# Where the low parts of the FFN operands are made, and in which order its weights are loaded

## The chip, the cores and the metric

One core of a Trainium2 chip runs the whole program. The metric is device time in microseconds (us) of one execution. The engines are named as in the profile: PE (TensorE) multiplies, DVE (VectorE), ACT (ScalarE) and POOL (GpSimd) work element by element, and SP (SyncE) only issues DMAs; POOL issues some too, through a queue of its own.

## What is computed

A trunk of two layers on x (1024 tokens by 1024 features), float32. Layer 0 mixes tokens with a gated DeltaNet, layer 1 with dilated-window attention; behind each mixer stands a SwiGLU block. Scale, shift and gate of each half layer come from a conditioning vector c.

```python
mod = (cond @ w_ada[layer] + b_ada[layer])
sh1, sc1, g1, sh2, sc2, g2 = jnp.split(mod[:, None, :], 6, axis=-1)
h = rms_norm(x, norm_mix[layer]) * (1.0 + sc1) + sh1
y = gated_deltanet_mixer(h, ...) if layer % 2 == 0 else dilated_attention_mixer(h, ...)
x = x + g1 * y
h = rms_norm(x, norm_ffn[layer]) * (1.0 + sc2) + sh2
gate, up = jnp.split(h @ w_ffn_in[layer], 2, axis=-1)     # 1024 x 2816 each
x = x + g2 * ((jax.nn.silu(gate) * up) @ w_ffn_out[layer])
```

## The kernel before

**Split numbers.** A float32 operand is held as a high part, rounded to the PE's 32-bit format by a copy on ACT, and a low part, the difference. One product of such operands is three matmuls (`split3`, `PE.then`, line L82 in the profile). `lo_of` (L164) makes the low parts. It counts its calls, and while `lo_pool` is 2 every second one goes to POOL, the others to DVE. `lo_pool` is 0 during the gated DeltaNet and 2 from the late part of layer 0's output projection (L1389) to the end.

**FFN-in.** The hidden size 2816 is 22 tiles of 128 columns, each with a gate part and an up part; the tokens are two halves of 512. A tile's four products (gate and up, by two halves) are made by a scheme of the Strassen kind with seven products, x = 1 to 7 (class `FfnIn`). Each of the seven is twelve matmuls of 128x128 by 128x512: four blocks of the feature sum by three. Its two operands are sums and differences: on the token side B[1] to B[7], made once per layer in `half0` (B[1], B[2]: the first 512 tokens) and `half1` (B[3] to B[7], which need the second 512 tokens); on the weight side made per tile in `weights`. Each of the operands has a high and a low part. A product is made in one of the PSUM banks "u", "y" and "v" (FFN-out's in "pd"). `taken` copies a finished product out of PSUM and adds it up; `column` makes silu(gate) times up of the second half; results go to the DRAM array `a_d`.

**The order of the products.** `begin` runs x=1 and x=2 of tiles 0, 1 and 2, which need the first tokens only. Inside it, behind the last product of tile 1, the norm's sums of the second tokens are reduced (`factors`: a product with ones into "pt", DVE at L347, and a short Newton step); behind the first product of tile 2 the factors are spread over the partitions by another small product and a copy (`row_bcast`, "rb", ACT at L306). Then `half1` multiplies the eight blocks of the second half by the row (L1157), scales and shifts them (ACT L1158), and forms B[3] to B[7]: the differences at L1174 and L1181 on DVE, two groups of four differences in place at L1177 and L1183 on POOL, and twenty operands with a high part (ACT L1151) and a low part (L164). `rest` runs the other products: for x in 3, 7, 6, 5, 4 tile 0 and tile 1 in turn (ten products), then tile by tile 7, 6, 2, 5, x=1 of the next tile, 3, 4. Meanwhile, in layer 0, every second product is followed by a piece of layer 1's conditioning (`mods1`): a DMA of 128x512 of `w_ada` ("araw"), and a multiply-add on DVE at L228 or L230.

**Weights.** A tile's two weight blocks of 128x1024 come by SP's queue into four buffers "wraw" (L1193), first used at the tile's first product in the text. Tile 2's first block, needed early, is loaded into a buffer of its own, "wr" (L1209). Its high part is made at L1215. Differences of blocks are at L1225 (POOL), L1226 and L1229 (DVE), the high parts of weight operands at L1198. `begin` makes the operands of (0,3), (1,3), (0,7) and (1,7) ahead of their products.

**FFN-out** (`ffn_out`) reads `a_d` back (L1343), in groups of 2, 4, 4, 4, 4 and 4 tiles, splits it (ACT L1345, L164), loads w_ffn_out (L1321), and adds each product times the gate to x (L1358), which in the first group is loaded from `xs_d` (L1354).

**What sets the order.** A scheduler puts each engine's instructions in an order from dependences and an estimate of their times; PE's in `begin` and `rest` are pinned to the order of the text. Each engine, and each DMA queue, then works in that order and waits where an input or a buffer is missing. So an instruction that waits holds all behind it on its engine.

Of the kernel before, what the change touches and what calls it, by code (L numbers as in the profile page):

```python
# [71 lines left out]
def trunk(tc, A, out, stop=None):  # L72
# [85 lines left out]
    cnt = [0]  # L158
    lo_pool = 2

    def lo_of(o, x, hi):
        cnt[0] += 1
        e = G if lo_pool and cnt[0] % lo_pool == 0 else V
        e.tensor_tensor(o, x, hi.bitcast(F32), ALU.subtract)  # L164
# [371 lines left out]
    with ExitStack() as ga:  # L536
# [4 lines left out]
        w_in = A["gdn_w_in"][0]  # L541
        lo_pool = 0
        wpools()
# [589 lines left out]
    class FfnIn:  # L1133
# [32 lines left out]
        def half1(self, xs, rb):  # L1166
            x0, x1, ft, sums = self.x0, xs, self.ft, self.sums
            for k in range(4, KT):
                self.h(k, x1[k], rb)
                self.B[3].append(self.pair(x1[k], False))  # L1170
            for k in range(4):
                self.h(k, x1[k], rb)
                t = sums.take()
                V.tensor_tensor(t, x1[k + 4], x1[k], ALU.subtract)  # L1174
                self.B[7].append(self.pair(t, True))
                sums.give(t)
                G.tensor_tensor(x0[k], x1[k], x0[k], ALU.subtract)  # L1177
                ft.give(x1[k])
            for k in range(4):
                t = sums.take()  # L1180
                V.tensor_tensor(t, x1[k + 4], x0[k], ALU.subtract)  # L1181
                self.B[6].append(self.pair(t, True))
                G.tensor_tensor(x0[k + 4], x0[k + 4], t, ALU.subtract)  # L1183
                sums.give(t)
                ft.give(x1[k + 4])
            for x, far, ts in ((5, True, x0[:4]), (4, False, x0[4:])):
                for t in ts:
                    self.B[x].append(self.pair(t, far))
                    ft.give(t)

        def raw(self, c0):
            r = self.raws()
            SP.dma_start(r.rearrange("p (k n) -> p k n", k=KT), rows_cols(A["w_ffn_in"][self.l], c0, P))  # L1193
            return r

        def op(self, x):
# [5 lines left out]
        def weights(self, i, x):  # L1202
            s, ft = self.st[i], self.sums
            if x in (1, 2):
                if x == 1:
                    if i == 2:

                        r = self.fw.tile([P, 1024], F32, name="wr", tag="wo")
                        SP.dma_start(r.rearrange("p (k n) -> p k n", k=KT),  # L1209
                                     rows_cols(A["w_ffn_in"][self.l], i * P, P))  # L1210
                    else:
                        r = s["rg"] = self.raw(i * P)
                        s["ru"] = self.raw(HID + i * P)
                    w = s["w"] = wps.tile([P, 2, 1024], F32R, name="w", tag="w")
                    ACT.activation(w[:, 0], r, AF.Copy)  # L1215
                    lo_of(w[:, 1], r, w[:, 0])
                c = slice((x - 1) * HALF, x * HALF)
                return s["w"][:, 0, c], s["w"][:, 1, c]
            if "rg" not in s:
                s["rg"], s["ru"] = self.raw(i * P), self.raw(HID + i * P)  # L1220
            a11, a12, a21, a22 = (t[:, j * HALF:(j + 1) * HALF] for t in (s["rg"], s["ru"]) for j in range(2))
            if x in (6, 5, 3) and "s1" not in s:
                t = self.fw.tile([P, 2, HALF], F32, name="ss", tag="wo")
                s["s1"], s["s2"] = t[:, 0], t[:, 1]
                G.tensor_tensor(s["s1"], a21, a22, ALU.add)  # L1225
                V.tensor_tensor(s["s2"], s["s1"], a11, ALU.subtract)  # L1226
# [47 lines left out]
        def column(self, i, g, where, x):  # L1274
# [3 lines left out]
            G.tensor_tensor(t, t, g, ALU.mult)  # L1278
            SP.dma_start(a_d[i, 1], t)
            where.give(g)  # L1280
            self.ft.give(t)

        def begin(self, factors, bcast):

            for i in range(3):
                self.product(i, 1)
# [3 lines left out]
                if i == 1:  # L1290
                    r = factors()
                    for j in ((0, 3), (1, 3), (0, 7), (1, 7)):
                        self.ops[j] = self.weights(*j)
# [39 lines left out]
    def ffn_out(l, ft, fw, raws, tail, between=None):  # L1333
# [4 lines left out]
        for gi, gn in enumerate(FG):  # L1338
            wo, acts = [], [[], []]
            for t in range(t0, t0 + gn):  # L1340
                for hf in range(2):
                    r = ft.take()
                    SP.dma_start(r, a_d[t, hf])  # L1343
                    hi, lo = hl_tile()
# [5 lines left out]
            for hf in range(2):  # L1350
                for n in range(KT):
                    if gi == 0:
                        xT[hf].append(ft.take())
                        SP.dma_start(xT[hf][n], xs_d[hf, n])  # L1354
                    o = pd()
# [32 lines left out]

    lo_pool, accs, araw = 2, None, 2  # L1389
    with ExitStack() as fa:  # L1390
# [48 lines left out]
        for kind in (1, 2):  # L1439
            pre.update(attn_products(0, 0, kind, range(2), hT, bank["p%d" % kind],  # L1440
                                     attn_weights(0, 0, kind, lambda ap, a: wtwo(fw, raws(), ap, a))))
        wcyc[0] = cycle([(wps, 1, (fw, "wraw", 4))])
        pre["w"] = attn_weights(0, 0, 0)
# [22 lines left out]
    with ExitStack() as da:  # L1466
# [200 lines left out]
        def half_done(hf):  # L1667
# [17 lines left out]
            stat = [Stat(None, *tmp[0:2]), Stat(None, *tmp[2:4])]  # L1685
            wpools(dw, 2, 2, 4)
            for h2, ns in ((0, range(KT)), (1, range(3)), (1, range(3, KT))):
                for n in ns:
# [93 lines left out]
```

## Time and profile before

| | us |
|---|---|
| median of 3 runs (lowest, highest) | 3025.17 (3014.49, 3026.26) |
| the profiled execution | 3023.1 |
| its span | 3021.3 |
| PE busy | 2799.0 |
| DVE busy | 1607.3 |
| ACT busy | 1067.9 |
| POOL busy | 998.1 |

In rows of windows each busy time is followed by the number of instructions; PEclk is the TensorE clock that was granted, as a share of full speed. The span is the time from the first to the last instruction of the profiled execution. An engine's busy time adds up its instructions. Stretches of the span by the profile: layer 0's late output projection and `begin` to the end of the ten products 820 to 935, its `rest` to 1330, its FFN-out 1330 to 1572; the same stages of layer 1 at 2280 to 2394, to 2750 and to the end, where the output phase overlaps the last products.

### The profile page before, as it was taken

Reading aid. Unit: us, or ns where it says so; the run is one execution under the profiler, and the core shown is the slowest. Engines: PE = TensorE matmul, PEld = TensorE weight load, DVE = VectorE, ACT = ScalarE, POOL = GpSimd, SP = SyncE. Lnnn points to the kernel's source line nnn. Section 1 sums busy time; section 2 is a strip of 40 time slices with the busy share of each in tenths; the row PEclk is TensorE's granted clock in tenths of the full one; section 3 lists DMA queues with packets and bytes.
Section 4 is the critical chain, followed back from the end, with each engine's and each line's share of the span. In section 5 each row is a group of like instructions: output and inputs, shape, how many; then the busy total and the mean of one; then the engine's idle time right before and its main releaser. Section 6 shows DMA issues by size and latency. Waiting matters only on the chain.

```text
span 3021.3 us, 40540 instructions
## 1 busy us (share of the span) xinstructions
PE 2799.0 (93%) x15303; PEld 2373.6 (79%) x15303; DVE 1607.3 (53%) x3055; ACT 1067.9 (35%) x2139; POOL 998.1 (33%) x866
## 2 busy tenths in 40 slices
PE   6889888898969999999999899999977899999999
PEld 5767777777757787877889799999966688887887
DVE  7875676656565555567455342333277633336443
ACT  5432333333443333332224453443335333334110
POOL 2141324332254343433224122322224633336220
PEclk8989999999989999999999999999968899999999
DMA  7333422236714433466212311111232222237211
GB/s 255 98 93 113 109 84 69 54 98 187 234 43 123 132 119 119 133 235 195 86 63 68 101 39 36 50 50 48 76 103 88 63 84 84 84 105 229 83 51 56
DMA packets 302208, 312.83 MB, mean 104 GB/s; under 512 B 34883, under 2 KB 219459, under 8 KB 302012
## 3 DMA queue, kind: packets, MB, share of 16 engines
q1 hardware_dynamic: 294444, 290.35, 31.3%
q0 software_dynamic: 7568, 19.89, 2.1%
q8 instruction: 120, 1.97, 0.3%
q14 instruction: 76, 0.62, 0.1%
HBM read 251.21 MB, written 63.66 MB: 104 GB/s over the span
## 4 chain that ended last, share of the span: by engine, by line
PE 67%; DVE 10%; DMA 10%; POOL 4%; issue 3%; ACT 3%; SPq 0%; DVEq 0%; POOLq 0%; ACTq 0%
PE pd L82 33%; PE u L82 13%; PE v L82 6%; PE pt L82 5%; DMA araw<-in_w_ada 4%; PE y L82 3%; PE ob L82 3%; POOL U L805 1%; POOL Ut L803 1%; PE pp L82 1%; DVE acc L230 1%; DMA wraw<-in_gdn_w_in 1%; PE sc L82 1%; DVE w L164 1%; DMA E<-gs_d 1%
## 5 line engine op out<-in xcount | busy, mean ns | idle before, releaser
L82 PE MATMUL pd<-hl,w 128*128 128x512 f32 x4248 | 1074.1, 406 | 32.4 <-ACT w L190 9.6
L82 PEld LDWEIGHTS pd<-hl,w 128*128 128x128 f32 x4248 | 801.4, 194 | 200.9 <-ACT w L190 10.5
L82 PE MATMUL pd<-w,hl 128*128 128x256 f32 x2880 | 377.0, 286 | 0.0
L82 PEld LDWEIGHTS pd<-w,hl 128*128 128x128 f32 x2880 | 355.3, 192 | 7.2 <-issue 6.0
L164 POOL TENSOR_TENSOR w<-wraw,w 128x512 fp32r<-128x512 f32 (+1 forms) x109 | 188.7, 1735 | 329.0 <-ACT w L190 159.0
L82 PE MATMUL u<-hx,wo 128*128 128x512 f32 x1056 | 261.7, 398 | 16.6 <-DVE wo L164 7.7
L82 PEld LDWEIGHTS u<-hx,wo 128*128 128x128 f32 x1056 | 202.8, 193 | 62.4 <-DVE wo L164 8.9
L164 DVE TENSOR_TENSOR w<-wraw,w 128x512 fp32r<-128x512 f32 (+1 forms) x169 | 152.8, 912 | 96.5 <-ACT w L190 72.7
L230 DVE SCALAR_TENSOR_TENSOR acc<-araw,vecT,acc 128x512 f32<-128x512 f32 x140 | 132.7, 948 | 109.1 <-DMA araw<-in_w_ada 108.6
L190 ACT ACTIVATE w<-wraw 128x512 fp32r<-128x512 f32 (+1 forms) x171 | 107.8, 645 | 218.3 <-DMA wraw<-in_gdn_w_in 101.3
L82 PE MATMUL u<-hl,w 128*128 128x512 f32 x528 | 133.2, 402 | 16.8 <-ACT w L1215 9.3
L142 POOL TENSOR_TENSOR ssa<-ssa,pw 128x8 f32<-128x8 f32 x48 | 80.7, 1683 | 170.1 <-DVE ssa L1536 160.7
L1358 DVE SCALAR_TENSOR_TENSOR qkv<-pd,modT,qkv 128x512 f32<-128x512 f32 x96 | 71.0, 747 | 117.8 <-PE pd L82 117.8
L82 PEld LDWEIGHTS u<-hl,w 128*128 128x128 f32 x528 | 102.2, 195 | 39.9 <-ACT w L1215 9.5
L82 PE MATMUL v<-hl,wo 128*128 128x512 f32 x528 | 127.4, 391 | 0.7 <-DVE ft L1257 0.7
L82 PE MATMUL u<-hl,wo 128*128 128x512 f32 x480 | 120.8, 402 | 7.7 <-ACT ft L1255 7.7
L82 PE MATMUL y<-hl,w 128*128 128x512 f32 x528 | 127.3, 390 | 0.0
L82 PE MATMUL v<-hx,wo 128*128 128x512 f32 x528 | 126.8, 390 | 0.1
L691 DVE SCALAR_TENSOR_TENSOR yv<-raw,vecT,yv 128x512 f32<-128x512 f32 x144 | 112.2, 779 | 14.0 <-ACT yv L689 13.0
L82 PEld LDWEIGHTS v<-hl,wo 128*128 128x128 f32 x528 | 99.4, 189 | 21.9 <-DVE ft L1257 1.1
L1578 DVE CUSTOM_DVE_ANT_0 p<-pt,bias 128x256 f32<-128x256 f32 (+1 forms) x192 | 61.6, 369 | 102.0 <-PE pt L82 63.4
L82 PEld LDWEIGHTS u<-hl,wo 128*128 128x128 f32 x480 | 92.5, 194 | 29.6 <-ACT ft L1255 9.9
(383 smaller groups left out, 4424.0 us busy)
## 6 DMA issues: line engine op xcount, KB each, us to landing
araw<-in_w_ada SPq DMA_DIRECT2D x160, 256.0 KB, 2.8
wraw<-in_w_ffn_in SPq DMA_DIRECT2D x66, 512.0 KB, 4.0
wraw<-in_dsw_w_in SPq DMA_DIRECT2D x68, 256.0 KB, 3.0
wraw<-in_w_ffn_out SPq DMA_DIRECT2D x34, 512.0 KB, 4.3
wraw<-in_gdn_w_in SPq DMA_DIRECT2D x66, 256.0 KB, 2.9
a_d<-ft SPq DMA_DIRECT2D x44, 256.0 KB, 2.0
ft<-a_d SPq DMA_DIRECT2D x44, 256.0 KB, 3.8
qkv<-in_w_ffn_in SPq DMA_DIRECT2D x22, 512.0 KB, 3.9
```

The lines of the kernel that those rows point to most:

```text
L82: i = f(*a, **k)
L142: G.tensor_tensor(o, i, pw[:, half, :n], ALU.pow)
L164: e.tensor_tensor(o, x, hi.bitcast(F32), ALU.subtract)
L190: ACT.activation(hi, raw, AF.Copy)
L230: V.scalar_tensor_tensor(acc, raw, condT[:, k:k + 1], acc, op0=ALU.mult, op1=ALU.add)
L691: V.scalar_tensor_tensor(yv, raw[:, i:i + HALF], convT[:, i, ct:ct + 1], yv, op0=ALU.mult, op1=ALU.add)
L803: G.tensor_tensor(t, U[:, 0:m, m:m + 1].to_broadcast([64, m, n]), U[:, m:m + 1, m + 1:32].to_broadcast([64, m, n]), ALU.mult)
L805: G.tensor_tensor(U[:, 0:m, m + 1:32], U[:, 0:m, m + 1:32], t, ALU.add)
L1358: V.scalar_tensor_tensor(xt, o, modT[:, l, 5, n:n + 1], xt, op0=ALU.mult, op1=ALU.add)
L1578: V.tensor_tensor_reduce(p_[i][:, hp, c0:], lg[i][:, hp * 256 + c0:hp * 256 + 256], bias[:, h, c0:], 1.0, -3.0e38, ALU.add, ALU.max, orow[ ...
```

## The change

Six things are done.

- `lo_pool` becomes a list, `aid_every`, and is no longer set to 2 at the late output projection of layer 0. So from there through FFN 0 and the first two kinds of attention weights (kinds 1 and 2) all low parts are on DVE. It is set to 2 before the weights of attention kind 0, and to 0 again before layer 1's output projection, so that FFN 1 has all of them on DVE too.
- The eight in-place differences of `half1` move from POOL to DVE (now L1179, L1182), the first four from the first loop to the second, beside their next use. For tiles 0 and 1 so does the sum at L1225.
- The loads of tiles 0 and 1 and "wr" are issued at the start of `begin`, through the helper `load`.
- `begin` makes four more weight operands ahead: (0,6), (1,6), (0,5), (1,5).
- The store of the second half of a tile's result, `a_d[i, 1]`, is issued on POOL's queue (SP's before): 22 per layer.
- In `ffn_out` the loads from `a_d` and `xs_d` are given priority in the scheduler.

```diff
-    lo_pool = 2
+    aid_every = [2]
     def lo_of(o, x, hi):
         cnt[0] += 1
-        e = G if lo_pool and cnt[0] % lo_pool == 0 else V
+        e = G if aid_every[0] and cnt[0] % aid_every[0] == 0 else V
...
-        lo_pool = 0
+        aid_every[0] = 0
...
                 self.B[7].append(self.pair(t, True))
                 sums.give(t)
-                G.tensor_tensor(x0[k], x1[k], x0[k], ALU.subtract)
-                ft.give(x1[k])
             for k in range(4):
                 t = sums.take()
+                V.tensor_tensor(x0[k], x1[k], x0[k], ALU.subtract)
                 V.tensor_tensor(t, x1[k + 4], x0[k], ALU.subtract)
                 self.B[6].append(self.pair(t, True))
-                G.tensor_tensor(x0[k + 4], x0[k + 4], t, ALU.subtract)
+                V.tensor_tensor(x0[k + 4], x0[k + 4], t, ALU.subtract)
                 sums.give(t)
-                ft.give(x1[k + 4])
+                ft.give(x1[k], x1[k + 4])
...
+        def load(self, i):
+            s = self.st[i]
+            if "rg" not in s:
+                s["rg"], s["ru"] = self.raw(i * P), self.raw(HID + i * P)
...
                     if i == 2:
-                        r = self.fw.tile([P, 1024], F32, name="wr", tag="wo")
-                        SP.dma_start(r.rearrange("p (k n) -> p k n", k=KT),
-                                     rows_cols(A["w_ffn_in"][self.l], i * P, P))
+                        r = s["wr"]
                     else:
-                        r = s["rg"] = self.raw(i * P)
-                        s["ru"] = self.raw(HID + i * P)
+                        self.load(i)
+                        r = s["rg"]
...
-                G.tensor_tensor(s["s1"], a21, a22, ALU.add)
+                (V if i < 2 else G).tensor_tensor(s["s1"], a21, a22, ALU.add)
...
-            SP.dma_start(a_d[i, 1], t)
+            G.dma_start(a_d[i, 1], t)
...
         def begin(self, factors, bcast):
+            for i in range(2):
+                self.load(i)
+            r = self.st[2]["wr"] = self.fw.tile([P, 1024], F32, name="wr", tag="wo")
+            SP.dma_start(r.rearrange("p (k n) -> p k n", k=KT), rows_cols(A["w_ffn_in"][self.l], 2 * P, P))
             for i in range(3):
...
-                    for j in ((0, 3), (1, 3), (0, 7), (1, 7)):
+                    for j in ((i, x) for x in (3, 7, 6, 5) for i in range(2)):
                         self.ops[j] = self.weights(*j)
...
-                    SP.dma_start(r, a_d[t, hf])
+                    with tc.high_priority():
+                        SP.dma_start(r, a_d[t, hf])
...
-                        SP.dma_start(xT[hf][n], xs_d[hf, n])
+                        with tc.high_priority():
+                            SP.dma_start(xT[hf][n], xs_d[hf, n])
...
-    lo_pool, accs, araw = 2, None, 2
+    accs, araw = None, 2
...
                              attn_weights(0, 0, kind, lambda ap, a: wtwo(fw, raws(), ap, a))))
+        aid_every[0] = 2
...
             wpools(dw, 2, 2, 4)
+            aid_every[0] = 0
```

**How it moves instructions.** SP's queue in layer 0, around the load of "wr". Before (w_out is the output projection's weight, "xt" the tokens of layer 0):

```order
L522 DMA xt<-xs_d 128x512 x7
L188 DMA wraw<-in_gdn_w_out 128x8x128 x3
L1193 DMA wraw<-in_w_ffn_in 128x8x128 x6
L1209 DMA wr<-in_w_ffn_in 128x8x128
L226 DMA araw<-in_w_ada 128x512
L1193 DMA wraw<-in_w_ffn_in 128x8x128 x2
L226 DMA araw<-in_w_ada 128x512 x2
```

With the change:

```order
L522 DMA xt<-xs_d 128x512 x7
L188 DMA wraw<-in_gdn_w_out 128x8x128 x2
L1289 DMA wr<-in_w_ffn_in 128x8x128
L188 DMA wraw<-in_gdn_w_out 128x8x128
L1192 DMA wraw<-in_w_ffn_in 128x8x128 x6
L226 DMA araw<-in_w_ada 128x512
L1192 DMA wraw<-in_w_ffn_in 128x8x128 x2
```

"wr" now stands ahead of all the w_ffn_in loads, and of the last one of the output projection.

DVE in layer 0, from the step that turns the reduced sums into factors (L347) into `half1`; "wo" are weight operands, "hl" and "hx" token operands. Before:

```order
L347 TENSOR_SCALAR ssx<-pt 128x4
L1229 TENSOR_TENSOR araw<-wraw 128x512
L164 TENSOR_TENSOR wo<-araw,wo 128x512
L1157 TENSOR_TENSOR xt<-xt,rb 128x512 x8
L1263 TENSOR_TENSOR ft<-y,ft 128x512
L164 TENSOR_TENSOR hl<-xt,hl 128x512
L1174 TENSOR_TENSOR araw<-xt 128x512 x2
L164 TENSOR_TENSOR hl<-xt,hl 128x512
L164 TENSOR_TENSOR hx<-araw,hx 128x512
L1174 TENSOR_TENSOR araw<-xt 128x512
L164 TENSOR_TENSOR hx<-araw,hx 128x512
```

With the change:

```order
L347 TENSOR_SCALAR ssx<-pt 128x4
L164 TENSOR_TENSOR wo<-araw,wo 128x512
L164 TENSOR_TENSOR wo<-ss,wo 128x512 x4
L1157 TENSOR_TENSOR xt<-xt,rb 128x512 x8
L1263 TENSOR_TENSOR ft<-y,ft 128x512
L164 TENSOR_TENSOR hl<-xt,hl 128x512 x2
L1174 TENSOR_TENSOR araw<-xt 128x512
L1179 TENSOR_TENSOR xt<-xt 128x512
L1174 TENSOR_TENSOR araw<-xt 128x512
L1179 TENSOR_TENSOR xt<-xt 128x512 x2
L164 TENSOR_TENSOR hl<-xt,hl 128x512
L1179 TENSOR_TENSOR xt<-xt 128x512
```

The five low parts of weight operands (the last four for x=6 and x=5) now stand ahead of the eight L1157, every low part is in DVE's row, and the differences of L1179 that were on POOL stand between those of L1174. On PE the products keep their order.

## Rows read from the trace of the kernel before

**Rows 1.** Windows: us; PE, PEld, DVE, ACT, POOL busy; PEclk; DMA share; GB/s.
```profile
820.00:935.00 115.00, 82.93 (x312) 63.77 (x311) 77.32 (x76) 51.18 (x81) 64.91 (x44) 0.82 0.24 74
935.00:1330.00 395.00, 384.17 (x1694) 316.35 (x1693) 218.07 (x279) 136.09 (x223) 159.28 (x101) 0.98 0.43 131
...
2280.00:2394.00 114.00, 85.38 (x321) 65.88 (x319) 83.78 (x84) 56.23 (x91) 65.31 (x46) 0.84 0.22 68
2394.00:2750.00 356.00, 356.00 (x1571) 294.86 (x1572) 130.22 (x190) 130.47 (x210) 142.90 (x97) 1.00 0.30 95
```

**Rows 2.** Timeline, TensorE, layer 0: start, duration, line, operation, count, [idle before <-releaser].
```profile
854.10 0.95 PE L82 MATMUL pt<-sq 128*128 128x1 f32 x8
862.78 1.22 PE L82 MATMUL u<-hl,w 128*128 128x512 f32 x2 [7.74 <-ACT w L1215]
865.20 3.88 PE L82 MATMUL u<-hl,w 128*128 128x512 f32 x10 [1.20 <-POOL w L164]
...
902.25 1.22 PE L82 MATMUL u<-hx,wo 128*128 128x512 f32 x2 [4.16 <-ACT wo L1198]
907.58 12.94 PE L82 MATMUL u<-hx,wo 128*128 128x512 f32 x46 [4.12 <-DVE wo L164]
...
926.81 2.88 PE L82 MATMUL v<-hx,wo 128*128 128x512 f32 x12
```

**Rows 3.** Timeline, SyncE's queue, layer 0, ahead of the row broadcast.
```profile
824.30 31.97 SPq L1193 DMA_DIRECT2D wraw<-in_w_ffn_in  x5
856.32 0.58 SPq L1209 DMA_DIRECT2D wr<-in_w_ffn_in  x1
```

**Rows 4.** Timelines, layer 0, behind the row broadcast: VectorE, GpSimd, ScalarE.
```profile
870.64 4.90 DVE L1157 TENSOR_TENSOR xt<-xt,rb 128x512 f32<-128x512 f32 x8 [13.41 <-ACT rb L306]
...
877.16 3.46 DVE L1174 TENSOR_TENSOR araw<-xt 128x512 f32<-128x512 f32 x2
...
876.65 6.78 POOL L1177 TENSOR_TENSOR xt<-xt 128x512 f32<-128x512 f32 x4
...
914.84 1.29 POOL L164 TENSOR_TENSOR wo<-ss,wo 128x512 fp32r<-128x512 f32 x1 [6.19 <-ACT wo L1198]
...
885.68 0.63 ACT L1151 ACTIVATE hx<-araw 128x512 fp32r<-128x512 f32 x1 [3.88 <-DVE araw L1174]
```

**Rows 5.** Timelines, layer 1, the same stretch: VectorE, GpSimd, TensorE.
```profile
2301.61 5.74 DVE L340 TENSOR_TENSOR qkv<-qkv 128x512 f32<-128x512 f32 x1
...
2322.19 0.16 DVE L347 TENSOR_SCALAR ssx<-pt 128x4 f32<-128x4 f32 x1
2333.15 4.90 DVE L1157 TENSOR_TENSOR qkv<-qkv 128x512 f32<-128x512 f32 x8 [10.80 <-ACT qkv L306]
...
2301.97 2.39 POOL L164 TENSOR_TENSOR w<-wraw,w 128x1024 fp32r<-128x1024 f32 x1
...
2308.76 4.44 PE L82 MATMUL u<-hl,w 128*128 128x512 f32 x12 [4.58 <-DVE qkv L490]
...
2386.76 3.00 PE L82 MATMUL v<-hx,wo 128*128 128x512 f32 x12
```

**Rows 6.** Layer-0 body: waits (us in total, times, longest), then VectorE and TensorE.
```profile
DVE acc L230 <- DMA araw<-in_w_ada: 60.0, 38, 3.3
...
PE u L82 <- ACT ft L1255: 8.4, 6, 2.2
...
1178.46 1.98 DVE L230 SCALAR_TENSOR_TENSOR acc<-araw,vecT,acc 128x512 f32<-128x512 f32 x1 [2.88 <-DMA araw<-in_w_ada]
...
1183.95 4.22 PE L82 MATMUL u<-hl,wo 128*128 128x512 f32 x12 [2.18 <-ACT ft L1255]
```

**Rows 7.** Timeline, TensorE, start of the output phases of layers 0 and 1.
```profile
1336.56 8.72 PE L82 MATMUL pd<-hl,w 128*128 128x512 f32 x25 [4.20 <-ACT hl L1345]
...
1405.29 5.74 PE L82 MATMUL pd<-hl,w 128*128 128x512 f32 x24 [2.17 <-DVE ft L1358]
...
2764.32 1.69 PE L82 MATMUL pd<-hl,w 128*128 128x512 f32 x6 [2.86 <-DVE qkv L1358]
```

More of the change, by code (lines that the diff above doesn't have):

```diff
@@ L1218, in weights @@
                 return s["w"][:, 0, c], s["w"][:, 1, c]
-            if "rg" not in s:
-                s["rg"], s["ru"] = self.raw(i * P), self.raw(HID + i * P)
+            self.load(i)
             a11, a12, a21, a22 = (t[:, j * HALF:(j + 1) * HALF] for t in (s["rg"], s["ru"]) for j in range(2))
@@ L1283, in begin @@
         def begin(self, factors, bcast):
+            for i in range(2):
+                self.load(i)
+            r = self.st[2]["wr"] = self.fw.tile([P, 1024], F32, name="wr", tag="wo")
+            SP.dma_start(r.rearrange("p (k n) -> p k n", k=KT), rows_cols(A["w_ffn_in"][self.l], 2 * P, P))
             for i in range(3):
```

## The prediction

> **What bounds the kernel now.** I read the page first, for the order of the engines: TensorE is the busy one, so a gain can only come from stretches in which it waits. Then the windows, cut at the borders of the stages the change touches [rows 1]. In the second layer's FFN-in proper TensorE has no gap: 1571 matmuls in 356.00 us, 0.2266 us each, so a product of 12 costs 2.72 us. In the stretches that lead into FFN-in it works 82.93 of 115 us at a granted clock of 0.82, and 85.38 of 114 at 0.84. At 0.2266 us the 312 matmuls of the first would take 70.7 us and the 321 of the second 72.7, so 44 and 41 us are lost there; the layer-0 body loses 395.00 − 384.17 = 11 as idle time. These 96 us, and some at the start of the output phases, are all that can be won.
>
> Next TensorE's own timeline through the first of these stretches [rows 2]. Two things are to be seen. Before the norm's factors can be broadcast, product (2,1) waits 7.74 us for its weight's high part and 1.20 for its low part; the broadcast is queued behind it. SyncE's rows say why [rows 3]: the load "wr", of which the high part is made, goes out at 856.32, behind five weight loads that hold the queue for 31.97 us as they wait for free buffers. From the arrival of the row broadcast (the first L1157 at 870.64, called R here; rows 4) the ten products of tiles 0 and 1 then follow the operands and end at 926.8, 56 us after R, where ten without waits take 27.2.
>
> **How VectorE and GpSimd share.** Eight L1157 take 4.90 us, 0.61 each, while GpSimd has nothing; two sums take 3.46, 1.73 each, while GpSimd runs four L1177 in 6.78, 1.70 each; a low part on GpSimd next to an idle VectorE takes 1.29 [rows 4]. So one op per 0.61 us becomes two per about 1.7: 0.85 us for each, slower than VectorE by itself. In layer 1 one L340 takes 5.74 us against a back-to-back run of GpSimd ops, the first of them 2.39 [rows 5].
>
> **A. Layer 0, "wr" before the weight loads: 10.8 us.** The order shows it ahead of the six FFN loads on SyncE. Its wait goes (7.74 + 1.20), and the product's two pieces, 1.22 and 3.88 after an idle spell, become one of 2.72 to 2.9 (2.2 less); I take 0.3 off for the wider low part on VectorE [rows 2]. Four more weight operands now stand ahead of the eight L1157. They are 4 × 0.61 = 2.4 us of VectorE in the gap in which it waits for the broadcast anyway; should that gap shrink to nothing they cost 2.4. Bounds 7 (the first wait alone) and 11.
>
> **B. Layer 0, from R to the end of the ten products: 16 us.** VectorE now has 8 L1157, 1 L1263, 16 sums and differences and 20 low parts: 45 operations, 45 × 0.61 = 27.5 us with no GpSimd beside it. In the kernel before the same 45 stood as 27 on VectorE and 18 on GpSimd. By the order the last low part for the x=6 products is the 39th: 23.8 us after R, plus 0.7 for the start, plus the five products still to come, 13.6: 38.1. I add 2 for a slow restart: the 46 matmuls behind the second gap took 12.94 us where 46 × 0.2266 is 10.4 [rows 2]. So 40 in place of 56. The waits of 4.16 and 4.12 us for weight operands go too, since those of x=6 and x=5 are made ahead; they are inside the 16. Lower bound 8 (those two waits alone); upper bound 23: eight L1157, one pair (1.2), then ten products with no wait make 33.3.
>
> **C, D. Layer 1, R earlier: 11 us.** There product (0,1) waits 4.58 us for an L490 that stands behind the blocked L340, and R comes 2333.15 − 2322.19 = 11.0 us after the statistic [rows 5]. After the change the statistic comes about 5 us sooner (5.74 − 0.61, with no GpSimd in the way), and R 4.8 after it: product 2.7, transposes and copy 2.1, as in A. Bounds 5 (one of the two) and 13.
>
> **E. Layer 1, from R to the end of the ten: 13.5 us.** 2386.76 − 2333.15 = 53.6 against the same 40 [rows 5]. Upper bound 20 (33.3 as in B); lower 4, half of layer 0's.
>
> **F.** The stores of a_d[i,1] leave SyncE for GpSimd's queue: 22 issues per layer on an engine that in the body works 159.28 of 395.00 us, and loses more than it gains [rows 1]. Nobody waits for a store until the output phase. 0, from −2 to 3.
>
> **G. Layer-0 body: 6 us, from −15 to 11.** VectorE waits 38 times for the conditioning weights' DMA, 60.0 us in all, at most 3.3 [rows 6]. Such an operation is queued ahead of the copies that free TensorE's banks. An example: VectorE idles 2.88 us, its L230 takes 1.98 beside a GpSimd op instead of under 1, a low part follows, and TensorE stands 2.18 us at 1183.95 [rows 6]. TensorE's waits of this kind are 6, 8.4 us in all. With no low parts on GpSimd the slow operations shrink, and I take back 6. Against it, three more low parts per tile queue on VectorE behind each DMA wait: 20 × 3 × 0.61 = 37 us of work, which VectorE's 395.00 − 218.07 us of idle time covers [rows 1], if it does not fall behind a wait. If a quarter of the 38 turns into a stall of 2.2 us that is 21, less the 6: −15. The upper bound is all of the idle. Layer 1 has no such DMA and no idle: 0.
>
> **H. Output phases: 9 us, from −4 to 12.** In layer 0 the first product waits 4.20 us and runs its 25 matmuls in 8.72 (5.67 at full clock, so 3.0 more); later there is a wait of 2.17; in layer 1 one of 2.86 [rows 7]. The priority leaves the layer-0 activation loads about where they were in SyncE's order (still behind the wraw loads), so I take half of the first 7.2, and the two small waits, which are on a sum (L1358) that GpSimd delays. The lower bound is one such load late by as much as the first wait, 4.2.
>
> The low parts of the late layer-0 projection and of two attention weight kinds also go to VectorE: 0 for the latter, where TensorE has no gap to win; the former is in A.
>
> **Sum.** 10.8 + 16 + 11 + 13.5 + 0 + 6 + 9 = 66.3. The profiled execution took 3023.1 us, so 2956.8; the median of the three runs, 3025.17, is 2.1 above it, so 2959.
>
> **Rivals.**
>
> 1. *The chain is bound by hand-overs, not by VectorE's throughput.* Sum on VectorE, high part on ScalarE, low part on VectorE, product: if the latencies of each hand-over set the pace, B gives only the two weight waits (8.3), A 7.7, D 5, and E, G, H nothing: 21 us, 3004. For it: ScalarE idles between the high parts, once for 3.88 us. Against it: what ends that idle is one of VectorE's long sums [rows 4], and several pairs may be in flight. Chance 0.10.
>
> 2. *GpSimd was worth its place.* If the two did not hinder each other, a split of the 45 would take 45 / (1/0.61 + 1/1.29) = 18.6 us, VectorE alone 27.5, so each layer's chain would grow by 9: B and E −9 each, C and G 0, A 10.8, D 5, H 9, and the whole −7: 3018, no change. Against it: 1.73 beside 1.70 where 0.61 and 1.29 stand alone [rows 4]. Chance 0.06. The Trainium skill speaks for this rival and against it in one place: "Perfetto Trace Analysis", section "Optimizing Scalar/DVE Operations", says that a saturated VectorE may hand work to GpSimd, but that they share a read port, so that it might not help; "SBUF — State Buffer", section "Who interferes with whom", says that an operation of VectorE with two inputs in SBUF contends with a GpSimd one that reads it. By the first half of the advice the time would be the 3018 of this rival; the trace's pairs of 0.61 and 1.73 agree with the second half.
>
> 3. *Slower: the queue behind the DMA waits.* In the layer-0 body each low part that used to escape to GpSimd now stands in VectorE's queue, behind the 38 waits for the conditioning weights. TensorE is held as soon as the operand of its next product is behind one. Price: 38 stalls of the size seen, 2.2 us, 84 us, in place of G's 6: 84 − 60.3 = +24, 3049. It makes the kernel slower where a wait costs TensorE more than 60.3 / 38 = 1.6 us on the mean, beyond the measurement's limit above 2.0. Against it: only 6 of 38 waits hold TensorE today, 1.4 us each [rows 6], and operands are made a product or more ahead. Chance 0.04.
>
> **How the numbers follow.** The forecast has 0.80. Its own terms err more upward in time than downward: G by 21, H by 13, E and B by 9 and 8; in quadrature some 28, so up to about 2987; downward some 11, so 2948. Gains in stretches I priced at nothing could make it 2932. Reaching up to 3000 takes in about half of rival 1; left out stay rivals 2 and 3 (0.10), the rest of rival 1 and the tails. A measurement of this kernel can tell 0.5%, 15 us, from no change: faster means below 3010. Forecast and rival 1 are faster, 0.90; rival 2 is the same, 0.06; rival 3 slower, 0.04.
>
> **What would show it.** A: no wait for "w" before the second transposes, and "wr" on SyncE ahead of the long row. B and E: VectorE's operations after R all at 0.6 to 0.7 us, the last product of tiles 0 and 1 some 40 us after R, and the windows' granted clock above 0.82 and 0.84. C: no L340 of 4 to 6 us. G: L230's wait for its DMA still near 60 us, but TensorE's wait for copies not longer than 8.4. H: the first output matmul waits under 4.2. Wrong it would be if the sums and low parts stay at 1.7 us with GpSimd idle, if R to the end stays above 50 us (rival 1), or if TensorE's idle time in the layer-0 body grows past 30 us (rival 3).

## The result and the profile after

The changed kernel takes 2953.6 us, median of 4 runs (2948.96 to 2955.79), against 3025.72 (3014.49 to 3027.67) of the kernel before, 4 runs: a ratio of 0.9767, 95% interval 0.974 to 0.9794, 72 us faster. Forecast were 2959, between 2932 and 3000. The profiled execution has a span of 2952.7 us; GpSimd is busy for 575.4 us in place of 998.1:

```profile
span 2952.7 us, 40358 instructions
...
PE 2779.0 (94%) x15303; PEld 2365.0 (80%) x15303; DVE 1684.1 (57%) x3333; ACT 1068.7 (36%) x2139; POOL 575.4 (19%) x632
```

TensorE's timeline cuts both spans into the same stages (R as in the prediction: the first L1157 behind the row broadcast; "end" is the end of the ten products of tiles 0 and 1).

| stage | before, us | after, us | gain | forecast |
|---|---|---|---|---|
| start to the late projection of layer 0 | 802.85 | 812.97 | -10.1 | 0 |
| to the reduction of the norm's sums | 51.25 | 46.24 | 5.0 | 0 |
| to R, layer 0 | 16.54 | 6.07 | 10.5 | 10.8 (A) |
| R to the end, layer 0 | 56.17 | 40.07 | 16.1 | 16 (B) |
| to the first output product | 409.75 | 395.01 | 14.7 | 9.6 (G, part of H) |
| to R, layer 1 | 996.59 | 980.55 | 16.0 | 13.2 (C, D, part of H) |
| R to the end, layer 1 | 53.61 | 40.74 | 12.9 | 13.5 (E) |
| to the end of the span | 634.54 | 631.05 | 3.5 | 2.9 (part of H) |
| sum | 3021.3 | 2952.7 | 68.6 | 66 |

The first line is not the change's: up to the late projection both programs are the same, instruction for instruction, and in the profiles of all the kernels below that point is reached between 800.20 and 813.59 us. Behind that point the two profiles differ by 78.7 us; the medians, for which that start is not known, differ by 72.

The windows of the lead-ins and bodies, cut near the same places of the program as those of before [rows 1] (columns as there):

```profile
823.00:915.00 92.00, 82.33 (x347) 65.50 (x346) 79.70 (x121) 56.09 (x89) 9.94 (x11) 0.94 0.41 121
915.00:1296.00 381.00, 377.27 (x1692) 312.82 (x1691) 243.03 (x340) 136.64 (x222) 64.18 (x57) 1.00 0.44 137
...
2238.00:2329.00 91.00, 77.59 (x325) 61.20 (x325) 75.99 (x119) 56.15 (x91) 10.74 (x15) 0.92 0.28 87
2329.00:2690.00 361.00, 361.00 (x1593) 298.88 (x1593) 193.34 (x256) 135.05 (x218) 59.94 (x57) 1.00 0.31 98
```

The 347 matmuls of the first take 92 us and not 115 for 312, and the granted clock is 0.94, not 0.82; in layer 1 0.92, not 0.84. TensorE in layer 0 [rows 2]:

```profile
859.21 0.95 PE L82 MATMUL pt<-sq 128*128 128x1 f32 x8
860.02 3.03 PE L82 MATMUL u<-hl,w 128*128 128x512 f32 x12
...
868.11 0.49 PE L82 MATMUL y<-hl,wo 128*128 128x512 f32 x1 [1.42 <-ACT hl L1151]
871.44 2.70 PE L82 MATMUL y<-hl,wo 128*128 128x512 f32 x6 [2.84 <-DVE hl L164]
...
888.32 11.04 PE L82 MATMUL u<-hx,wo 128*128 128x512 f32 x48
...
905.35 2.88 PE L82 MATMUL v<-hx,wo 128*128 128x512 f32 x12
```

Product (2,1) now stands right behind the reduction, in one piece of 3.03 us; nothing waits for "w". The waits of 4.16 and 4.12 are gone: 48 matmuls of x=6 and x=5 run in one piece of 11.04. What is left are waits for the first high and low parts, 1.42 and 2.84 us among them. The end comes at 905.35. SyncE's queue [rows 3]: "wr" goes out at 822.38, ahead of the row of six loads that holds the queue for 34.33:

```profile
822.38 3.43 SPq L1289 DMA_DIRECT2D wr<-in_w_ffn_in  x1
...
827.64 34.33 SPq L1192 DMA_DIRECT2D wraw<-in_w_ffn_in  x6
```

VectorE behind R [rows 4], and the end of its work for x=6:

```profile
865.28 4.91 DVE L1157 TENSOR_TENSOR xt<-xt,rb 128x512 f32<-128x512 f32 x8
...
872.51 0.68 DVE L1179 TENSOR_TENSOR xt<-xt 128x512 f32<-128x512 f32 x1
873.11 0.68 DVE L1174 TENSOR_TENSOR araw<-xt 128x512 f32<-128x512 f32 x1
...
889.07 0.69 DVE L164 TENSOR_TENSOR hx<-araw,hx 128x512 fp32r<-128x512 f32 x1
```

The operations, moved sums (L1179) too, take 0.68 and follow each other after 0.60; the last low part for x=6 begins 23.8 us after R, as forecast, though it is the 40th operation and not the 39th. The same stretch of layer 1 [rows 5], VectorE and then TensorE:

```profile
2275.50 0.15 DVE L347 TENSOR_SCALAR ssx<-pt 128x4 f32<-128x4 f32 x1
2280.91 4.90 DVE L1157 TENSOR_TENSOR qkv<-qkv 128x512 f32<-128x512 f32 x8 [5.26 <-ACT qkv L306]
...
2321.65 2.88 PE L82 MATMUL v<-hx,wo 128*128 128x512 f32 x12
```

From the statistic to R it is 5.4 us instead of 11.0, and no L340 of layer 1 takes more than 0.69. In the layer-0 body [rows 6], waits, and then TensorE's last stall of size:

```profile
DVE acc L230 <- DMA araw<-in_w_ada: 44.9, 35, 2.9
...
PE u L82 <- ACT ft L1255: 6.8, 2, 3.7
...
1291.26 4.62 PE L82 MATMUL u<-hl,wo 128*128 128x512 f32 x12 [3.73 <-ACT ft L1255]
```

VectorE waits for the conditioning's DMA 44.9 us in 35 waits, in place of 60.0 in 38 [rows 6]; the prediction had named "near 60" as a sign, and this one did not come. TensorE waits for the copies twice. The output phases [rows 7], layer 0 and layer 1:

```profile
1300.36 40.83 PE L82 MATMUL pd<-hl,w 128*128 128x512 f32 x168 [1.76 <-ACT hl L1351]
...
2696.93 1.66 PE L82 MATMUL pd<-hl,w 128*128 128x512 f32 x6 [0.65 <-DVE qkv L1365]
```

### The profile page after: what moved, and what is told of

It is laid out like the page before. It is cut to its first block, busy times and chain, and to the rows that moved or that the text cites. A ratio compares the mean times of both kernels' runs of the same rounds, so it can differ in the third digit from the quotient of the medians.

```text
span 2952.7 us, 40358 instructions
## 1 busy us (share of the span) xinstructions
PE 2779.0 (94%) x15303; PEld 2365.0 (80%) x15303; DVE 1684.1 (57%) x3333; ACT 1068.7 (36%) x2139; POOL 575.4 (19%) x632
## 4 chain that ended last, share of the span: by engine, by line
PE 61%; DVE 6%; DMA 4%; ACT 1%; issue 1%; POOL 0%; SPq 0%; DVEq 0%; ACTq 0%; POOLq 0%
PE pd L82 29%; PE u L82 14%; PE v L82 7%; PE y L82 4%; PE pt L82 2%; PE ob L82 2%; PE pp L82 1%; PE tq L82 1%; DMA gl<-og_d 1%; DVE w L164 1%; DVE hl L164 1%; DMA b_d<-v_d 1%; DMA wraw<-in_w_ffn_in 1%; DVE wo L164 0%; PE p L82 0%
## 5 line engine op out<-in xcount | busy, mean ns | idle before, releaser
L164 DVE TENSOR_TENSOR w<-wraw,w 128x512 fp32r<-128x512 f32 (+1 forms) x243 | 201.4, 840 | 107.2 <-ACT w L190 74.6
L82 PE MATMUL u<-hx,wo 128*128 128x512 f32 x1056 | 253.2, 390 | 4.7 <-ACT ft L1255 3.1
L230 DVE SCALAR_TENSOR_TENSOR acc<-araw,vecT,acc 128x512 f32<-128x512 f32 x140 | 109.9, 785 | 92.8 <-DMA araw<-in_w_ada 92.1
L1365 DVE SCALAR_TENSOR_TENSOR qkv<-pd,modT,qkv 128x512 f32<-128x512 f32 x96 | 71.6, 749 | 122.7 <-PE pd L82 122.7
L164 DVE TENSOR_TENSOR wo<-ss,wo 128x512 fp32r<-128x512 f32 x88 | 83.7, 957 | 91.8 <-ACT wo L1202 90.2
L1225 POOL TENSOR_TENSOR ss<-wraw 128x512 f32<-128x512 f32 x30 | 41.8, 1392 | 382.6 <-PE u L82 361.3
L82 PEld LDWEIGHTS v<-hx,wo 128*128 128x128 f32 x528 | 99.0, 188 | 20.6
```

What stands on the lines that cost most here:

```text
L82: i = f(*a, **k)
L230: V.scalar_tensor_tensor(acc, raw, condT[:, k:k + 1], acc, op0=ALU.mult, op1=ALU.add)
L1225: (V if i < 2 else G).tensor_tensor(s["s1"], a21, a22, ALU.add)
L1365: V.scalar_tensor_tensor(xt, o, modT[:, l, 5, n:n + 1], xt, op0=ALU.mult, op1=ALU.add)
```

## The experiments

Times are medians; "to R" and "R to the end" are stages of the table, of layer 0 first. Each ratio is to runs of the kernel before on the same chip. Stages that a kernel leaves alone vary from profile to profile: the body between 393.6 and 398.5, R to the end in layer 0 between 38.9 and 42.3. Smaller differences are not read.

| kernel | us | ratio to before, interval | to R, 0 | R to end, 0 | body, 0 | R to end, 1 |
|---|---|---|---|---|---|---|
| before | 3025.7 | | 16.5 | 56.2 | 409.8 | 53.6 |
| changed | 2953.6 | 0.9767 (0.974, 0.9794) | 6.1 | 40.1 | 395.0 | 40.7 |
| loads alone | 3008.4 | 0.9937 (0.9917, 0.9958) | 6.9 | 56.8 | 407.1 | 52.1 |
| VectorE alone | 2971.1 | 0.9824 (0.9807, 0.9841) | 15.0 | 49.9 | 394.1 | 42.8 |
| four operands late | 2967.8 | 0.9812 (0.9792, 0.9832) | 5.4 | 50.9 | 395.8 | 44.9 |
| eight sums on GpSimd | 2959.2 | 0.9786 (0.9772, 0.9801) | 6.1 | 45.0 | 398.5 | 43.8 |
| body's low parts shared | 2968.4 | 0.9813 (0.9796, 0.983) | 6.1 | 38.9 | 411.5 | 41.2 |
| all low parts shared | 2995.0 | 0.9908 (0.9888, 0.9928) | 7.3 | 48.6 | 407.2 | 43.2 |
| no priority | 2952.7 | 0.9767 (0.9748, 0.9786) | 6.1 | 40.1 | 397.9 | 41.5 |
| store on SyncE | 2951.0 | 0.9768 (0.9753, 0.9782) | 6.1 | 39.8 | 399.0 | 40.9 |
| attention on VectorE too | 2954.2 | 0.9773 (0.9757, 0.979) | 6.1 | 42.3 | 393.6 | 41.2 |
| first order by hand | 2957.2 | 0.9783 (0.976, 0.9805) | 8.2 | 44.5 | 393.6 | 42.1 |
| second | 2953.6 | 0.9771 (0.9755, 0.9788) | 6.1 | 43.8 | 396.5 | 39.7 |
| third | 2951.9 | 0.9766 (0.9742, 0.9789) | 6.1 | 43.1 | 394.0 | 38.7 |

**The loads alone.** The kernel before with

```diff
         def begin(self, factors, bcast):
+            for i in range(2):
+                self.load(i)
+            r = self.st[2]["wr"] = self.fw.tile([P, 1024], F32, name="wr", tag="wo")
+            SP.dma_start(r.rearrange("p (k n) -> p k n", k=KT), rows_cols(A["w_ffn_in"][self.l], 2 * P, P))
```

> The kernel before with one part of the change: the loads of tiles 0 and 1 and of wr are issued at the start of begin; all else as before. Theory 1 (VectorE and GpSimd hinder each other, and the loads are one separate part): from the first transposes to R in layer 0 falls from 16.5 us to about 8 (the 7.74 us wait goes, the low part on GpSimd stays late by about 1.2), R to the end of the ten products stays at 56 and 53.6; in layer 1 some 2 us; in all 10 us, about 3015. Theory 2 (the order of loads and operands is what counts): R to the end shrinks too, in all 20 us or more, 3005 or less.

TensorE of this kernel, layer 0:

```profile
855.61 1.16 PE L82 MATMUL pt<-sq,ssx 128*128 128x128 f32 x8 [1.22 <-POOL ssx L142]
...
889.05 1.22 PE L82 MATMUL u<-hx,wo 128*128 128x512 f32 x2 [5.12 <-ACT wo L1203]
894.39 13.59 PE L82 MATMUL u<-hx,wo 128*128 128x512 f32 x46 [4.12 <-DVE wo L164]
...
914.22 2.88 PE L82 MATMUL v<-hx,wo 128*128 128x512 f32 x12
```

The way to R falls by 9.7 us, R to the end not at all: the 5.12 and 4.12 for late weight operands stand. Theory 1 holds. In layer 1 the way from the statistic to R fell from 10.96 to 4.41 us, more than the 2 expected, and the whole is 18 us faster than its runs of before, not 10.

**VectorE alone.** The kernel before with `aid_every` set as in the change and the moved sums in `half1` and at L1225.

> The kernel before with another part alone: low parts, the eight in-place sums and the first sums of tiles 0 and 1 on VectorE as in the changed kernel; loads, store, priority and the four weight operands as before. Theory 1: operations of VectorE behind R take 0.6 to 0.7 us each, R to the end falls from 56 to about 45 and from 53.6 to about 43 (some of the waits for late weight operands stay), R comes 5 us earlier in layer 1, the layer-0 body loses 6 us or more: 35 us in all, about 2990. Theory 2: with all work on one engine and the same order R to the end stays above 50, the time stays within 15 us of 3025. If GpSimd had been worth its place: R to the end above 56, time above 3025.

TensorE of this kernel, layer 0:

```profile
858.40 5.20 PE L82 MATMUL u<-hl,w 128*128 128x512 f32 x12 [7.31 <-ACT w L1214]
...
890.60 1.22 PE L82 MATMUL u<-hx,wo 128*128 128x512 f32 x2 [3.22 <-ACT wo L1197]
893.30 12.35 PE L82 MATMUL u<-hx,wo 128*128 128x512 f32 x46 [1.48 <-DVE wo L164]
...
915.10 2.89 PE L82 MATMUL v<-hx,wo 128*128 128x512 f32 x12
```

The wait for "wr" is there (7.31), R to the end is 49.9 and 42.8, the body 15.7 us shorter, the late projection 5.3: 2971, 20 us better than expected, most of it in places that had been priced at 6 and at nothing. Theory 2 falls: the order was nearly that of before. (The 49.9 is just under the 50 named for it; the time fell by 56 us and not by under 15.)

**The four operands late.**

```diff
-                    for j in ((i, x) for x in (3, 7, 6, 5) for i in range(2)):
+                    for j in ((i, x) for x in (3, 7) for i in range(2)):
```

> The changed kernel without the four weight operands of x=6 and x=5 made ahead. The prediction put the two waits of 4.16 and 4.12 us for them inside its term B: R to the end in layer 0 grows from 40 to about 48 (49.9 where all work was on VectorE and these operands were late), in layer 1 from 41 to about 43: 10 us slower, about 2964. Rival: they are ready in time in any case, nothing changes, 2954.

TensorE of this kernel, layer 0:

```profile
887.49 0.73 PE L82 MATMUL u<-hx,wo 128*128 128x512 f32 x2 [2.75 <-ACT wo L1202]
890.19 13.14 PE L82 MATMUL u<-hx,wo 128*128 128x512 f32 x46 [1.96 <-DVE wo L164]
...
908.51 4.61 PE L82 MATMUL v<-hl,wo 128*128 128x512 f32 x12 [2.46 <-DVE ft L1257]
```

R to the end grows by 10.9 and 4.2 us, the whole by 14. The waits are 2.75 and 1.96 us, and a third, 2.46, comes behind them; the 46 matmuls take 13.14 where 46 x 0.2266 is 10.4, the 12 behind the third 4.61.

The parts do not add up. Without the four operands the kernel is at 0.9812 of before, and VectorE alone is at 0.9824: on top of the engine's move, the early loads (18 us by themselves), the store and the priority leave no gain that can be told, although R comes 9.6 us sooner in layer 0 and 6.6 in layer 1. Where that goes, the rows do not show; with the four operands the whole is 72 us.

**The eight sums on GpSimd.** `V` back to `G` in the two lines of `half1`.

> The changed kernel with only the eight in-place sums of half1 back on GpSimd, at their new places. Theory 1: each sum on GpSimd runs beside VectorE at about 1.7 us and costs a VectorE operation some 1.1 us more, 8 x 1.1 = 8.8 against 8 x 0.61 = 4.9 saved, and products of x=6 wait for a slower engine: R to the end 44 us or more in place of 40, in all 8 us slower, about 2961. If a small share on GpSimd is worth it: R to the end about 36, 8 us faster, about 2946.

VectorE and then GpSimd of this kernel, layer 0:

```profile
863.11 1.28 DVE L164 TENSOR_TENSOR hl<-xt,hl 128x512 fp32r<-128x512 f32 x2
864.32 1.28 DVE L1174 TENSOR_TENSOR araw<-xt 128x512 f32<-128x512 f32 x2
...
869.49 1.76 DVE L1174 TENSOR_TENSOR araw<-xt 128x512 f32<-128x512 f32 x1
...
863.17 9.22 POOL L1179 TENSOR_TENSOR xt<-xt 128x512 f32<-128x512 f32 x4 [8.04 <-ACT xt L1158]
```

4.9 and 3.1 us more, 2959: theory 1, a little cheaper than said. While VectorE runs without a gap its operations keep to 0.64, and GpSimd's four sums stretch over 9.22 us; once GpSimd has come in, VectorE's take 1.76.

**The body's low parts shared.**

```diff
+        aid_every[0] = 2
         ff.rest(mods1)
+        aid_every[0] = 0
```

> The changed kernel with every second low part of layer 0's rest (the body after half1) on GpSimd again; begin, half1, the output phases and layer 1 as changed. Theory 1 (the 2.2 us stalls of the body came from contention): the layer-0 body takes 6 us or more longer again, about 2960. Rival 3 of the prediction (low parts queued behind the DMA waits hold TensorE): the body gets shorter than in the changed kernel, by 5 us or more, about 2948.

TensorE's waits in the body, and two of the stalls:

```profile
PE u L82 <- ACT ft L1255: 17.5, 9, 4.4
...
974.17 4.62 PE L82 MATMUL u<-hl,wo 128*128 128x512 f32 x12 [2.18 <-ACT ft L1255]
...
1119.08 3.01 PE L82 MATMUL u<-hl,wo 128*128 128x512 f32 x12 [2.19 <-ACT ft L1255]
```

The body is 16.5 us longer, as long as before the change. TensorE's waits for the copies are 17.5 us in place of 6.8. Rival 3 has the sign wrong: low parts on VectorE behind 35 DMA waits do no harm, and sharing does. The run does not part the two ways in which it may: an L230 takes 1.05 us on the mean in place of 0.81, beside GpSimd, and a low part made from "wraw" takes 1.33 on GpSimd where VectorE takes 0.69.

**All low parts shared**, from the late projection on:

```diff
+    aid_every[0] = 2
     accs, araw = None, 2
...
-            aid_every[0] = 0
```

> The changed kernel with every second low part on GpSimd again from the late projection of layer 0 to the end (sums, loads, four operands, store and priority as changed). Theory 1 (VectorE and GpSimd hinder each other): R to the end of the ten products grows from 40 to about 48 in both layers, the layer-0 body from 395 to about 411 as with the body alone shared, the way to R in layer 1 by 7: some 40 us slower than the changed kernel, about 2993. If GpSimd is worth its place for low parts: R to the end 36 to 40, no slower than 2954.

2995: 41 us of the 72 are lost, in the late projection (51.0 us, as before the change), R to the end in layer 0, the body, and 17 us ahead of layer 1's statistic. In layer 1 R to the end grew by 2.5 only, not by 8.

**No priority, and the store on SyncE.** Each one line of the change undone.

> The changed kernel without the priority for the loads of the output phase. The prediction gave it some 3 of the 9 us of its term H: the layer-0 output phase with its start 3 us longer, 2957. Rival (the sums of the output phase gained because GpSimd is silent, the priority brings nothing): no difference, 2954.

> The changed kernel with the stores of a_d[i,1] on SyncE's queue again. The prediction gave the move 0 (-2 to 3): no difference, 2954, layer-0 body 395 as changed. Rival (on SyncE a store waits for its data ahead of the loads of weights and conditioning, which then come late): the layer-0 body some 5 us longer, 2959.

2952.7 and 2951.0: neither makes a difference that can be measured. The body of the second is 399.0, half a microsecond above those that have the store on GpSimd; the rival's 5 us don't show.

**The attention on VectorE too.**

```diff
-        aid_every[0] = 2
         wcyc[0] = cycle([(wps, 1, (fw, "wraw", 4))])
```

> The changed kernel with the low parts of the attention's remaining weights on VectorE too (34 of 128x512 leave GpSimd). The prediction's reason for 0 in the attention is that TensorE has no gap there that these operations set: no difference, 2954. Rival (contention costs wherever the two engines meet): the stage from the first attention product to the statistic of layer 1 some 5 us shorter, 2949.

2954.2, and from the first output product to the statistic of layer 1 975.36 us against 975.14: sharing shows no cost in a stage in which TensorE does not wait for these operations.

**Three orders by hand.** `half1` rewritten: every step its own instruction, kept in the order of the text on VectorE and ScalarE. First order, in short:

```python
for n in range(4):                 # x=3: scale, high, low of block n+4, next product by the row
    scale(ks[n]); p = hi_of(x1[ks[n]], False); lo(x1[ks[n]], p); mul(ks[n + 3])
for k in range(4):                 # x=7: scale, difference, high, first sum; low part one k later
for k in range(4):                 # x=6: the same
```

> The changed kernel with half1 written in an order by hand and kept in it on VectorE and ScalarE: the first token operands behind three products by the row instead of eight, each low part one step behind its high part, the differences for x=7 ahead of the sums for x=6 and so on. Theory 1 with VectorE's throughput as the bound: the last low part for x=6 is the 35th instead of the 39th operation, 35 x 0.61 = 21.4 us, plus 0.7 and 13.6: R to the end about 36 in place of 40 in each layer, 9 us faster, about 2945. If hand-overs bound the chain: 40 as before, 2954.

R came 2.1 us later, as the pinned chain waited for an older addition; the products of x=3 ended earlier, and each difference for x=7 then waited for its scaling: 44.5 and 42.1. The last low part for x=6 was the 39th operation, not the 35th, and began 25.7 us after R. In the second order all scalings come first, and the chain's first instruction is free:

> The changed kernel with half1 in a second order by hand on VectorE and ScalarE: products by the row and low parts of x=3 in turn, then all scalings, then differences and low parts for x=7 and x=6 with one or two operations between a high part and its low part; the first instruction on either engine is left free, so that the chain does not wait for an older one. The first such order won some 7 us on the x=3 products and lost them where each difference waited for the scaling before it. If VectorE's throughput is the bound: R to the end about 37 in place of 40 in each layer, 6 us faster, about 2948. If the hand-overs between ScalarE and VectorE bound it: 40 or more, 2954 or slower.

TensorE of this kernel, layer 0:

```profile
869.26 3.48 PE L82 MATMUL y<-hl,wo 128*128 128x512 f32 x14 [0.23 <-DVE hl L1176]
...
879.39 3.48 PE L82 MATMUL v<-hx,wo 128*128 128x512 f32 x14 [1.09 <-DVE hx L1176]
...
886.99 9.60 PE L82 MATMUL u<-hx,wo 128*128 128x512 f32 x41 [1.57 <-DVE hx L1176]
...
901.16 4.61 PE L82 MATMUL v<-hl,wo 128*128 128x512 f32 x12 [1.85 <-DVE ft L1307]
```

VectorE runs almost without a gap from R (busy 24.4 us of the 25.1 up to the last low part for x=6); x=3 and x=7 are done sooner, but the last low part for x=6 came behind three for x=4, and TensorE, in pieces, ends no earlier in layer 0: 43.8. Layer 1 wins 1.0. Both orders come out nearer to what the expectations had named for hand-overs (40 or more) than to the 36 and 37 of VectorE's throughput; but in the second VectorE idles for 0.7 us only up to that low part. The third order keeps those three low parts behind:

> The changed kernel with half1 in a third order by hand: as the second, and the low parts for x=5 and x=4 kept behind the last one for x=6. In the second order VectorE ran without a gap, the last low part for x=6 was the 42nd operation, 25.2 us after R, and the ten products ended 18.6 us later. If the count of VectorE's operations ahead of that low part sets the end, it is now the 37th, 37 x 0.61 = 22.6 us, and R to the end 41 in place of 43.8 in layer 0; against the changed kernel (40) no gain: 2954 give or take 3. If the order inside does not matter: 43.8 as in the second.

TensorE of this kernel, layer 0:

```profile
889.16 11.07 PE L82 MATMUL u<-hx,wo 128*128 128x512 f32 x48
...
905.27 4.62 PE L82 MATMUL v<-hl,wo 128*128 128x512 f32 x12 [2.32 <-DVE ft L1308]
```

The last low part for x=6 begins 23.6 us after R, 1.5 sooner than in the second order and no sooner than in the changed kernel, and layer 1 ends at 38.7, 2.0 better than the change; layer 0 at 43.1 where 41 were expected, because the additions behind the products are late (the wait of 2.32 us, then 12 matmuls in 4.62). 2951.9 (2945.95 to 2959.41): no version found is measurably faster than the changed kernel.

## Why the prediction was right

**The bound.** The 44, 41 and 11 us named as all that could be won were the right places, and two others were left out: 5.0 us in the late projection, which the prediction put "in A" at nothing, and in the body the matmuls that run slower behind a stall, since its 11 us are idle time alone.

**A, C, D.** 10.8 forecast, 10.5 measured; the loads alone give 9.7 of it. For C and D the statistic was to come 5 us sooner and R 4.8 behind it. From the first attention product to the statistic it is 6.7 us less, and R comes 5.41 behind it: 12.2 together against 11. The first of the two is partly luck: from the first attention product to the statistic the changed kernel takes 728.4 us, the other kernels that leave this stretch alone 729.6 to 733.4, the kernel before 735.1. The loads alone give the second (4.41), VectorE alone the first: from the first output product to the statistic 971.85 us, before 985.63, with the loads alone 984.43.

**B, E.** 40 us from R to the end were forecast for both layers, 40.07 and 40.74 came. Of the 16.1 in layer 0, VectorE alone gives 6.2, the four operands 10.9 when they come on top of all the rest; in layer 1 10.9 and 4.2. The prediction held the chain on VectorE to be most of it and the waits for weight operands, 8.3, to be inside: the sum was right, the shares in layer 0 lean to the operands. That it fell on 40 is partly luck: the 2 us added for a slow restart went elsewhere. The 48 matmuls of x=6 and x=5 run at full clock in 11.04; 1.3 us go to the rest of the product that was under way when the last low part was done (at 889.76), and 0.7 to the wait of 0.40 ahead of the tenth product and the slower matmuls behind it. The count of VectorE's operations is only part of what sets when the last operand for x=6 is there: in the second order by hand it is the 40th operation (not the 42nd, as the third order's expectation has it) and begins 25.1 us after R, in the third the 37th, at 23.6; but in the changed kernel the 40th begins at 23.8, as there is less idle time ahead of it. The end hangs on what follows as well, where layer 0 lost up to 4 us again.

**F.** 0 forecast, no difference measured.

**G, the mis-sized term.** 6 us with a start of the output phase of 3.6; 14.7 came for both. (The other kernels that make the body's low parts on VectorE take 393.6 to 399.0 us for this stage, the two with the body of before 407.1 and 409.8, so the gain is some 8 to 16.) TensorE's waits in the body fell from 12.9 to 6.8 us, which is the 6 that the term had taken back, and the first output product's from 4.20 to 1.76. Then there is what a stall costs behind its end: three products after stalls took 4.61, 4.22 [rows 6] and 5.16 us where a product in a row takes 2.88, and one does now, 4.62: 3.6 us. The last 2.6 lie within what the stage varies by. Why such a product is slow, the granted clock shows (kernel before; us; PE busy; PEclk; DMA share; GB/s):

```profile
1000.45:1005.06 4.61, 4.61 (x13) 0.63 0.30 88
1142.41:1145.45 3.04, 3.04 (x13) 1.00 0.00 0
1320.77:1325.93 5.16, 5.16 (x13) 0.55 0.96 372
```

In the first and the third stretch the clock was at the lower of its two levels (1.2 of 2.4 GHz, 0.5) for much of the time; in the second, behind a stall as long as that of the first, it was at the upper one throughout. The step that failed is that G priced a stall at its idle time alone, where B and H had counted slow matmuls. Rival 3 and the lower bound of -15 had the wrong sign, as the shared body shows.

**H.** 2.4 at the start of layer 0's output phase, 3.8 from there to the first attention product (250.5 to 246.7) and 3.5 in layer 1: 9.7, forecast 9, but not by the priority, which gives nothing by itself. The waits for the additions at L1358 (now L1365), 2.17 and 2.86 [rows 7], are 0 and 0.65. With all low parts shared they are at most 0.71 and 2.45, but 0.98 and 1.94 with the store on SyncE: that GpSimd had delayed these additions is not shown.

**The rivals.** Rival 1 (hand-overs) would have left R to the end near 48 and the body as it was; it is 40.07 and 40.74, and the engine alone takes 10.9 us off it in layer 1 and 15.7 off the body. Rival 2 (GpSimd worth its place) would have made the shared kernels no slower than the change: they are 5.5, 15 and 41 us slower. That 2959 came within 6 us of 2953.6 has luck in it: terms that were too small, 5 us each in the late projection and the body, stand against first 800 us that were 10.1 us slower in this profile; whether they were in the other executions is not known. Why one and the same program reaches the late projection up to 13 us later in one execution than in another was not looked into.

## What to carry to other kernels

Before work is shared between VectorE and GpSimd, look in the trace at one operation's time with the other engine idle and busy: if 0.61 and 1.29 become 1.7 and 1.7, one engine by itself is faster, but it pays only in stretches where TensorE waits for it. Then ask what its queue holds ahead of the next operand, and make the operands that TensorE wants next there first: from R to the end in layer 0 four of them gave 10.9 us on top of the rest, the engine's move by itself 6.2. Measure the parts together, too: here the early loads gave 18 us by themselves and nothing that can be told on top of the engine's move without those four. Price a stall of TensorE at its idle time plus the matmuls behind it that run at a lower granted clock.

## What was not expected of the hardware

- Who holds whom differed between two cases. In the kernel with the eight sums on GpSimd the first of four took 4.18 us and the four 9.22, while VectorE went on at 0.64; in the kernel before a single L340 on VectorE took 5.74 against a run of GpSimd [rows 5]. The Trainium skill, "SBUF — State Buffer", section "Who interferes with whom", says that the order of issue, not the shape of an operation, decides who is blocked. These two agree as to the shape: both of the operations held are of 128x512. They do not settle the order: by the recorded starts VectorE was first in both, at 863.11 against 863.17 and at 2301.61 against 2301.97.
- Stalls of nearly equal length are followed by matmuls of different length: before the change one of 2.20 us (at 1142.41) by 12 matmuls in 3.04 us, another of 2.18 (at 1000.45) by 12 in 4.61. The granted clock was 1.00 behind the first and 0.63 behind the second; why it fell in one place and not in the other, no run here shows.
